# Diffusion backbone with experts: evictions of narrow expert runs queued behind the next wide unit's splits, and regrouped small runs in the mixers

## The chip, the cores and the metric

One core of a Trainium2 chip. The metric is the device time of one execution in microseconds (us); less is better. Engine names are those of the profile: PE is TensorE's matmuls, PEld its weight loads, DVE is VectorE, ACT is ScalarE, POOL is GpSimd, SP is SyncE, whose queue issues the transfers of weights.

## What is computed

Two layers over 256 latent and 256 context tokens of width 1024, float32. Each layer: three token mixers on the same modulated input, gated and merged, then a feed-forward part, dense in layer 0 and eight experts with two per token in layer 1.

```python
def token_mixer(h_lat, h_ctx, lp, need_ctx):
    ...
    out_l = merge_branches(h_lat @ w_gate, (ssd_l, na_l, conf_l)) @ lp['w_o']

def ssd_direction(xs, bm, cm, dt_raw, a_log, dt_bias, h0, reverse):
    ...
    dt = jax.nn.softplus(dt_raw.astype(jnp.float32) + dt_bias.astype(jnp.float32))
    a = -jnp.exp(a_log.astype(jnp.float32))
    y, h = ssd_scan(xs, dt, a, bm, cm, h0)

def moe_swiglu(h, w_router, w_gate, w_up, w_down):
    logits = (h @ w_router).astype(jnp.float32)
    top_v, top_i = lax.top_k(logits, TOP_K)
    top_w = jax.nn.softmax(top_v, axis=-1)
    combine = jnp.sum(jax.nn.one_hot(top_i, N_EXPERTS, ...) * top_w[..., None], axis=-2)
    out = combine[..., 0:1] * swiglu(h, w_gate[0], w_up[0], w_down[0])
    for e in range(1, N_EXPERTS):
        out = out + combine[..., e:e + 1] * swiglu(h, w_gate[e], w_up[e], w_down[e])
    return out
```

## The kernel before

**Big matmuls.** Weights stream from memory through staging buffers on SP's queue (five of 1 MB in the expert stage) and are split into two parts in `split` (L113): ScalarE copies the high part `h_...` (L116), VectorE subtracts to get the low part `l_...` (L117). Three buffers of each are in turn. TensorE then makes three products, high by high, high by low, low by high. In the mixers and the dense feed-forward these are L205 to L207 and L251 to L253, in the experts L1546.

**What sets the order.** The program is written in Python generators and a scheduler with priorities sets each engine's queue. The mixers' small work (attention, the state space part SSD, the conformer convolution, the sums of the conditioning `ada`) runs in jobs that are pumped (`pump`, `spawn`) between the big matmuls: each `yield x` says how much of the big stream shall pass before the job goes on. `defer` keeps a closure of matmuls back for two steps, so that ScalarE and VectorE have made its operands, and `behind()` puts its issue after the last big matmul. Small products take their PSUM tiles from a pool `pw` of four buffers.

**The stages.** Mixers of layer 0 up to about 720 us, dense feed-forward to 1085, mixers of layer 1, routing to 1550, experts from 1550 to 2340 us.

**The mixers' parts.** `dt_path` makes the time steps `dt` of both directions: eight slices of the width, three products each (L865 to L867), with 32 columns. `ada_v` sums conditioning weights on VectorE (`adac`, L374) and then adds up partitions on TensorE with four small matmuls (L382). `attention` transposes the probabilities `P` to `PT` (closure `turned`, a head and a block of queries at a time) and multiplies with the values (`values`). `states` makes SSD chunk states, one direction a closure. `ssd_y` has three closures: `diag` (`ydS`, L1063, masks `MS` from ScalarE L1054 to L1055 and VectorE L1056), `off` (`yoS`, L1080, with `ES` from a DMA and an exponential, L1077) and `fin`.

**The experts.** `moe` (L1294) alternates two generators. `wide()` runs experts 0 to 3 through `expert` and `stream`: units of 1 MB of weights, each split in two halves (`h_er` and so on; tiles `e`, `er` for gate and up, `ed`, `edr` for down). `narrow()` runs experts 4 to 7, up to 64 tokens each, through `expert64` with unsplit float32 weights: runs `nn` (gate and up, L1428) of four units, 32 matmul records in the trace, then down projections `ndn` (L1453). Four narrow units alternate with two wide ones. At the end of an `nn` run ScalarE evicts it to `ntn` (L1433), TensorE transposes that to `npn` (L1438), ScalarE takes a Silu (`nsn`, L1441) and VectorE multiplies (`hnn`, L1443). After the last `ndn` the result is split (`ynHn`, `ynLn`) and combined by `ncn` (L1465). The eviction is issued right behind the run; transposes and what follows wait in the list `later`, which `flush` runs after the next wide unit is issued:

```python
            for _ in islice(w, m):
                self.flush()
```

Of the kernel before, what the change touches and what calls it, by code (L numbers as in the profile page):

```python
# [53 lines left out]
class Body:  # L54
# [298 lines left out]
    def ada_v(self, l, g):  # L353
# [6 lines left out]
        for j0 in (0, 2):  # L360
            accs = []
            for j in (j0, j0 + 1):
# [3 lines left out]
                for k in range(KD):  # L366
# [8 lines left out]
                    yield 0.7 * len(streams)  # L375
                    if j == 1 and k == 0:
                        self.keep()

            ps = self.pw(f"ada{l}{g}{j0}")
            for s in streams:  # L380
                for j, acc in zip((j0, j0 + 1), accs):
                    nc.tensor.matmul(ps[32 * j:32 * j + 32], self.con("oc")[:, 1 - s:33 - s], acc[:, s * 512:(s + 1) * 512],  # L382
                                     start=(s == streams[0]), stop=(s == 1), skip_group_check=True)
# [333 lines left out]
    def attention(self, l, q, kT, v, nt, o_):  # L717
# [4 lines left out]
        q_ = []  # L722
        for q0, nk, lat in streams:
            nkb = nk // 128
            for hp in range(4):
# [5 lines left out]
                def turn(P, j, qb, PT=PT, nm=nm, nk=nk, nkb=nkb, st=st):  # L731

                    nc.vector.tensor_scalar(P, P, st[:, j, qb, 5:6], None, op0=ALU.mult)

                    def turned():
                        if not PT:
                            PT.update({i: self.t4(f"PT{nm}{i}").rearrange("p (k t) -> p k t", t=256) for i in range(2)})
                        pt = self.pw(f"PT{nm}{j}{qb}")
                        for kb in range(nkb):
                            nc.tensor.transpose(pt[:, kb * 128:(kb + 1) * 128], P[:, kb * 128:(kb + 1) * 128], self.con("id"))  # L740
                        ev = nc.scalar.copy if j else nc.vector.tensor_copy
                        ev(PT[j][:, :nkb, qb * 128:(qb + 1) * 128], pt[:, :nk].rearrange("p (k t) -> p k t", t=128))
                    self.defer(q_, turned)
                if lat:
                    for qb in range(2):
# [17 lines left out]
                        for j in range(2):  # L763
                            turn(P[j], j, qb)
                            yield 1.7
                else:
# [6 lines left out]
                    for j in range(2):  # L773
# [5 lines left out]
                        for qb in range(2):  # L779
                            turn(P[j][:, qb * 256:(qb + 1) * 256], j, qb)  # L780
                        yield 1.5
# [7 lines left out]
                self.defer(q_, values)  # L789
                yield 0.5  # L790
        yield from self.undefer(q_)

# [61 lines left out]
    def dt_path(self, l):  # L854
# [3 lines left out]
        wH = self.t2("wdtH" + nm, F32R)[:, :KD * 32].rearrange("p (k n) -> p k n", k=KD)  # L858
# [157 lines left out]
    def ssd_y(self, nm, b, hin, q_):  # L1016
# [23 lines left out]
        for g in range(G):  # L1040
# [6 lines left out]
            for r in range(2):  # L1047
                load(*((1, g) if r == 0 else (0, g + 1)))
                pb = cb[r, g]
                for hq in range(2):  # L1050
# [7 lines left out]
                    def diag(r=r, hq=hq, M=M, g=g, xd=xd, st=st):  # L1058
                        if "pd" not in st:
                            st["pd"] = self.pw(f"yd{nm}{b}{g}")  # L1060
# [751 lines left out]
```

## Time and profile before

| | us |
|---|---|
| median of 3 runs (2364.26 to 2365.93) | 2364.38 |
| the profiled execution's own time | 2367.87 |
| its span, first to last instruction | 2366.1 |
| PE busy, 0 to 720 / 720 to 1085 | 675.64 / 354.72 |
| PE busy, 1085 to 1550 / 1550 to 2340 | 435.05 / 751.12 |
| mean granted clock of TensorE, of full speed | 0.978 |

The page sums the engines over the whole span; the stages differ, so the busy times of TensorE by stage stand beside it. Matmuls are pipelined: a matmul's record is longer than the step to the next one, so the chain of waits, which counts from start to start, gives the price of one in a stream. "Idle before, releaser" in a group of instructions says what an engine waited for ahead of that group; it matters only where the engine is on the chain.

### The profile page before, as it was taken

Reading aid. Unit: us, or ns where it says so; the run is one execution under the profiler, and the core shown is the slowest. Engines: PE = TensorE matmul, PEld = TensorE weight load, DVE = VectorE, ACT = ScalarE, POOL = GpSimd, SP = SyncE. Lnnn points to the kernel's source line nnn. Section 1 sums busy time; section 2 is a strip of 40 time slices with the busy share of each in tenths; the row PEclk is TensorE's granted clock in tenths of the full one; section 3 lists DMA queues with packets and bytes.
Section 4 is the critical chain, followed back from the end, with each engine's and each line's share of the span. In section 5 each row is a group of like instructions: output and inputs, shape, how many; then the busy total and the mean of one; then the engine's idle time right before and its main releaser. Section 6 shows DMA issues by size and latency. Waiting matters only on the chain.

```text
span 2366.1 us, 29723 instructions
## 1 busy us (share of the span) xinstructions
PE 2226.4 (94%) x11075; PEld 1632.5 (69%) x11075; DVE 1509.5 (64%) x2384; ACT 1030.1 (44%) x1658; POOL 17.4 (1%) x32
## 2 busy tenths in 40 slices
PE   7999999699999999999999889899999989999897
PEld 3776677477777777788877779766655656566564
DVE  3667999787667665536898765743433555565556
ACT  4334673643342222225347685443332345454453
POOL 0000000000000000000000000000000000000000
PEclk9999999899999999999999999999999999999998
DMA  7232253445445556423423344488888899999995
GB/s 269 95 117 72 76 172 127 116 156 169 147 143 160 173 175 199 147 98 102 147 89 104 107 146 161 139 324 330 341 320 320 330 365 375 357 385 347 348 370 206
DMA packets 123658, 492.51 MB, mean 208 GB/s; under 512 B 12784, under 2 KB 23792, under 8 KB 89712
## 3 DMA queue, kind: packets, MB, share of 16 engines
q1 hardware_dynamic: 122656, 487.89, 57.4%
q10 hardware_dynamic: 848, 2.62, 0.3%
q8 instruction: 89, 1.46, 0.2%
q14 instruction: 65, 0.53, 0.1%
HBM read 488.24 MB, written 2.23 MB: 207 GB/s over the span
## 4 chain that ended last, share of the span: by engine, by line
PE 71%; issue 11%; DVE 7%; DMA 6%; ACT 4%; POOL 0%; SPq 0%; POOLq 0%; DVEq 0%; ACTq 0%
PE er L1546 8%; PE nn L1428 7%; PE e L1546 4%; DMA adaw<-in_ada_w_dram 4%; PE ndn L1453 4%; PE edr L1546 3%; PE ed L1546 2%; PE wg L205 2%; PE wg L207 2%; PE wg L206 2%; DVE adac L374 2%; PE xbcL L205 1%; PE xbcL L206 1%; PE xbcL L207 1%; PE fu L206 1%
## 5 line engine op out<-in xcount | busy, mean ns | idle before, releaser
L374 DVE SCALAR_TENSOR_TENSOR adac<-adaw,sc,adac 128x512 f32<-128x512 f32 x224 | 160.1, 747 | 57.3 <-DMA adaw<-in_ada_w_dram 56.7
L117 DVE TENSOR_TENSOR l_er<-r_er,h_er 128x1024 fp32r<-128x1024 f32 x132 | 154.5, 1218 | 59.9 <-ACT h_er L116 59.5
L1428 PE MATMUL nn<-r_ngun,xn 128*64 128x512 f32 (+1 forms) x768 | 168.2, 561 | 0.0
L116 ACT ACTIVATE h_er<-r_er 128x1024 fp32r<-128x1024 f32 x132 | 133.0, 1053 | 42.2 <-DMA r_er<-in_moe_gu_dram 29.4
L205 PE MATMUL wg<-hHm,h_wg 128*128 128x512 f32 (+1 forms) x384 | 135.7, 355 | 1.8 <-ACT g L682 1.1
L206 PE MATMUL wg<-hLm,h_wg 128*128 128x512 f32 (+1 forms) x384 | 129.9, 339 | 0.0
L207 PE MATMUL wg<-hHm,l_wg 128*128 128x512 f32 (+1 forms) x384 | 128.8, 339 | 0.5 <-DVE l_wg L117 0.4
L1546 PE MATMUL er<-h_er,gHp 128*128 128x512 f32 (+1 forms) x288 | 110.5, 389 | 17.7 <-ACT h_er L116 17.7
L1428 PEld LDWEIGHTS nn<-r_ngun,xn 128*64 128x64 f32 x768 | 54.2, 137 | 91.9 <-issue 85.1
L1546 PE MATMUL er<-h_er,gLp 128*128 128x512 f32 (+1 forms) x288 | 108.1, 381 | 0.0
L117 DVE TENSOR_TENSOR l_e<-r_e,h_e 128x1024 fp32r<-128x1024 f32 x44 | 52.2, 1222 | 63.5 <-ACT h_e L116 62.6
L1453 PE MATMUL ndn<-r_ndn,hnn 128*64 128x512 f32 x352 | 87.4, 598 | 0.0
L572 DVE SCALAR_TENSOR_TENSOR ccv<-cu,cols,ccv 128x488 f32<-128x488 f32 (+14 forms) x120 | 84.5, 729 | 1.0
L1443 DVE TENSOR_TENSOR hnn<-npn,nsn 128x256 f32<-128x256 f32 (+1 forms) x24 | 9.6, 401 | 117.6 <-ACT nsn L1441 117.6
L1433 ACT ACTIVATE ntn<-nn 128x512 f32<-128x512 f32 (+1 forms) x24 | 13.5, 561 | 162.7 <-PE nn L1428 162.7
L1546 PE MATMUL er<-l_er,gHp 128*128 128x512 f32 (+1 forms) x288 | 84.3, 381 | 0.0
L205 PEld LDWEIGHTS wg<-hHm,h_wg 128*128 128x128 f32 x384 | 72.7, 189 | 14.5 <-issue 4.0
L1546 PEld LDWEIGHTS er<-h_er,gHp 128*128 128x128 f32 x288 | 54.8, 190 | 40.2 <-ACT h_er L116 29.0
L116 ACT ACTIVATE h_wg<-r_wg 128x1024 fp32r<-128x1024 f32 x48 | 50.6, 1058 | 71.8 <-PE wg L206 52.0
L117 DVE TENSOR_TENSOR l_edr<-r_edr,h_edr 128x1024 fp32r<-128x1024 f32 x66 | 77.0, 1217 | 4.4 <-ACT h_edr L116 4.1
L207 PEld LDWEIGHTS wg<-hHm,l_wg 128*128 128x128 f32 x384 | 72.2, 189 | 10.1 <-DVE l_wg L117 2.1
L206 PEld LDWEIGHTS wg<-hLm,h_wg 128*128 128x128 f32 x384 | 72.8, 190 | 8.8 <-issue 2.3
(642 smaller groups left out, 5955.5 us busy)
## 6 DMA issues: line engine op xcount, KB each, us to landing
r_ngun<-in_moe_gu_dram SPq DMA_DIRECT2D x88, 1024.0 KB, 7.1
r_er<-in_moe_gu_dram SPq DMA_DIRECT2D x66, 1024.0 KB, 7.3
r_ndn<-in_moe_down_dram SPq DMA_DIRECT2D x44, 1024.0 KB, 7.6
adaw<-in_ada_w_dram SPq DMA_DIRECT2D x160, 256.0 KB, 3.1
r_edr<-in_moe_down_dram SPq DMA_DIRECT2D x33, 1024.0 KB, 7.4
r_wg<-in_w_in_dram SPq DMA_DIRECT2D x48, 512.0 KB, 3.6
r_e<-in_moe_gu_dram SPq DMA_DIRECT2D x22, 1024.0 KB, 7.6
cbS<-csd SPq DMA_DIRECT2D x24, 512.0 KB, 4.9
```

Source lines behind the costliest of these rows:

```text
L116: nc.scalar.activation(Hd, src, AF.Copy)
L117: nc.vector.tensor_tensor(Ld, src, Hd.bitcast(F32), op=ALU.subtract)
L205: mm(out, wh, xh, start=(first and kk == 0), stop=False, skip_group_check=True)
L206: mm(out, wh, xl, start=False, stop=False, skip_group_check=True)
L207: self.last = mm(out, wl, xh, start=False, stop=(kk == kc - 1), skip_group_check=True).ins
L374: nc.vector.scalar_tensor_tensor(d, w, c, d, op0=ALU.mult, op1=ALU.add)
L572: nc.vector.scalar_tensor_tensor(y[:, :, a:b], x[:, :, a + s:b + s], w[:, k:k + 1], y[:, :, a:b], op0=ALU.mult, op1=ALU.add)
L1428: mm(ps[64 * h:64 * h + 64, :n], x[kk], w[:, h, k, :], start=(kk == 0), stop=(kk == KD - 1), skip_group_check=True)
L1433: nc.scalar.activation(t, ps[:, :n], AF.Copy)
L1443: nc.vector.tensor_tensor(d, v[:, :, 1], g, op=ALU.mult)
L1453: mm(ps[64 * h:64 * h + 64], hT[:, kk * 64:(kk + 1) * 64], w[:, h, k, :], start=(kk == 0), stop=(kk == fc - 1), skip_group_check=True)
L1546: mm(ps[s][j], st[kk], w[p][:, k, :], start=(kk == 0 and p == 0 and q == 0), stop=(kk == kc - 1 and p == 1), skip_group_check=True)
```

## The change

In the experts, the evictions `ntn` and the split of `ynHn`, `ynLn` become closures in a list `evicts`. `stream` runs them behind the second half's split of the next wide unit (`lastH`, set in `split`); `flush` now issues the transposes behind the last wide matmul so far (`last`, set in `stream`). In the mixers, `dt_path` packs high and low weights into 64 columns and makes two products in place of three; `ada_v` waits some more steps before its sums and issues them behind the last big matmul; `attention` transposes both heads in one closure and puts the values with the next one; `states` does both directions in one closure; `ssd_y` has one closure for a direction, which holds what were `diag`, `off` and `fin`; these are kept back one step and not two.

```diff
-        nc.scalar.activation(Hd, src, AF.Copy)
+        self.lastH = nc.scalar.activation(Hd, src, AF.Copy).ins
...
-                    yield 0.7 * len(streams)
+                    yield 0.64 * len(streams)
...
+            yield len(streams)
             ps = self.pw(f"ada{l}{g}{j0}")
-            for s in streams:
-                for j, acc in zip((j0, j0 + 1), accs):
-                    nc.tensor.matmul(ps[32 * j:32 * j + 32], self.con("oc")[:, 1 - s:33 - s], acc[:, s * 512:(s + 1) * 512],
+            with self.behind():
+                for s in streams:
+                    for j, acc in zip((j0, j0 + 1), accs):
+                        nc.tensor.matmul(ps[32 * j:32 * j + 32], self.con("oc")[:, 1 - s:33 - s], acc[:, s * 512:(s + 1) * 512],
...
+                        pts = [self.pw(f"PT{nm}{j}{qbs[0]}") for j in range(2)]
+                        n = len(qbs) * 128
+                        for f in joined:
+                            f()
+                        joined.clear()
...
+                    self.defer(q_, turned, 1)
...
-            nc.tensor.matmul(ps[0:32, :], wH[:, k, :], self.h[0][k], start=(k == 0), stop=False)
-            nc.tensor.matmul(ps[0:32, :], wH[:, k, :], self.h[1][k], start=False, stop=False)
-            nc.tensor.matmul(ps[0:32, :], wL[:, k, :], self.h[0][k], start=False, stop=(k == KD - 1))
+            nc.tensor.matmul(ps[0:64, :], wp[:, k, :], self.h[0][k], start=(k == 0), stop=False, skip_group_check=True)
+            nc.tensor.matmul(ps[0:32, :], wp[:, k, 0:32], self.h[1][k], start=False, stop=(k == KD - 1), skip_group_check=True)
...
+        nc.vector.tensor_tensor(b3(x), pt[:, :, 1], bc(self.col("dtb")), op=ALU.add)
+        nc.vector.tensor_tensor(b3(x), pt[:, :, 0], b3(x), op=ALU.add)
...
+                def state(g=g, xe=xe):
+                    ps = {r: self.pw(f"st{nm}{b}{r}{g}") for r in dirs}
...
+                self.defer(q_, state, 1)
+                yield 1.8 * len(dirs)
...
+                def diag(r=r, M=M, g=g, xd=xd, st=st, E=E):
+                    if r == 0:
+                        st["pd"] = self.pw(f"yd{nm}{b}{g}")
+                    E = {d: e.rearrange("p i l -> p (i l)") for d, e in E.items()}
+                    for e in E.values():
+                        nc.scalar.activation(e, e, AF.Exp)
+                    for hl in range(8):
+                        nc.tensor.matmul(st["pd"][64 * (hl % 2):64 * (hl % 2) + 64, (hl // 2) * 128:(hl // 2 + 1) * 128],
...
+                    po = {d: self.pw(f"yo{nm}{b}{g}{d}") for d in E}
...
+                self.defer(q_, diag, 1)
+                yield 1.8 if r == 0 else 4.2
...
             for _ in islice(w, m):
-                self.flush()
+                self.flush(self.last)
+            self.evict()
...
+    def evict(self, ins=None):
+
+        f, self.evicts = self.evicts, []
+        if f:
+            with self.tc.issue_after(ins) if ins is not None else ExitStack():
+                for g in f:
+                    g()
...
                 if (i + 1) * nk == KD:
+                    self.evict()
                     self.flush()
                     t = self.t2(f"nt{nm}{c}")[:, :n]
-                    with self.prio("ev"):
-                        nc.scalar.activation(t, ps[:, :n], AF.Copy)
+
+                    def evicted(t=t, ps=ps, n=n):
+                        with self.prio("ev"):
+                            nc.scalar.activation(t, ps[:, :n], AF.Copy)
+                    self.evicts.append(evicted)
...
                     w = self.weight(None, f"{name}{i}_{s}", t=t[:, s * 1024:(s + 1) * 1024])
+                if s:
+                    self.evict(self.lastH)
```

How the order of instructions moves, at three places. The first is ScalarE's queue around the end of the narrow run `nn70`, the stop at 2115 us in the trace. `h_er242` and `h_er243` are the high halves of the next two wide units, `ntn70` is the eviction. Before:

```order
L116 ACTIVATE hHr2_15825<-etr230_16307 128x512
L1433 ACTIVATE ntn70_16395<-nn70_16370 128x512
L1441 ACTIVATE nsn70_16424<-npn70_16419 128x256
L116 ACTIVATE h_er242_0_16399<-r_er242_16397 128x1024
L116 ACTIVATE h_er242_1_16409<-r_er242_16397 128x1024
L116 ACTIVATE h_er243_0_16429<-r_er243_16427 128x1024
L116 ACTIVATE h_er243_1_16441<-r_er243_16427 128x1024
```

After:

```order
L116 ACTIVATE hHr2_15793<-etr230_16275 128x512
L116 ACTIVATE h_er242_0_16366<-r_er242_16364 128x1024
L116 ACTIVATE h_er242_1_16376<-r_er242_16364 128x1024
L1466 ACTIVATE ntn70_16363<-nn70_16338 128x512
L116 ACTIVATE h_er243_0_16397<-r_er243_16395 128x1024
L116 ACTIVATE h_er243_1_16409<-r_er243_16395 128x1024
L1475 ACTIVATE nsn70_16392<-npn70_16387 128x256
```

The eviction moved from ahead of the splits of unit 242 to behind both of them.

The same place in TensorE's queue, before:

```order
L1428 MATMUL nn70_16370<-r_ngun71_16377,xn_12733 64x512 x4
L1428 MATMUL nn70_16370<-r_ngun72_16383,xn_12733 64x512 x4
L1428 MATMUL nn70_16370<-r_ngun73_16389,xn_12733 64x512 x4
L1438 MATMUL npn70_16419<-con_t_98,ntn70_16395 128x128 x4
L1546 MATMUL er240_0_16314<-h_er242_0_16399,gHp0_14651 128x512
L1546 MATMUL er240_0_16314<-h_er242_0_16399,gLp0_14652 128x512
L1546 MATMUL er240_0_16314<-h_er242_0_16399,gHp0_14651 128x512
```

After:

```order
L1458 MATMUL nn70_16338<-r_ngun73_16357,xn_12701 64x512 x4
L1586 MATMUL er240_0_16282<-h_er242_0_16366,gHp0_14619 128x512
L1586 MATMUL er240_0_16282<-h_er242_0_16366,gLp0_14620 128x512
L1586 MATMUL er240_0_16282<-h_er242_0_16366,gHp0_14619 128x512
L1586 MATMUL er240_0_16282<-h_er242_0_16366,gLp0_14620 128x512
L1586 MATMUL er241_0_16283<-h_er242_1_16376,gHp0_14619 128x512
L1586 MATMUL er241_0_16283<-h_er242_1_16376,gLp0_14620 128x512
L1586 MATMUL er240_0_16282<-l_er242_0_16367,gHp0_14619 128x512 x2
L1586 MATMUL er241_0_16283<-h_er242_1_16376,gHp0_14619 128x512
L1586 MATMUL er241_0_16283<-h_er242_1_16376,gLp0_14620 128x512
L1586 MATMUL er241_0_16283<-l_er242_1_16377,gHp0_14619 128x512 x2
L1472 MATMUL npn70_16387<-con_t_98,ntn70_16363 128x128 x4
```

The transposes `npn70` moved from the end of the narrow run to behind unit 242's first twelve rows, which now follow the run at once.

The third place is TensorE's queue at the layer 0 conformer's output product `wb0conf_out`, around 450 to 465 us; `ydS` are products of `ssd_y`, `ada010` the row sums. Before:

```order
L1063 MATMUL ydS020_3352<-MS02010_3345,xdS0201_3269 64x128 x4
L1063 MATMUL ydS020_3352<-MS02011_3383,xdS0201_3269 64x128 x4
L1063 MATMUL ydS021_3555<-MS02100_3484,xdS0210_3478 64x128 x4
L382 MATMUL ada010_3621<-adac010_2977,con_t_98 32x512
L382 MATMUL ada010_3621<-adac011_3328,con_t_98 32x512
L382 MATMUL ada010_3621<-adac010_2977,con_t_98 32x512
L382 MATMUL ada010_3621<-adac011_3328,con_t_98 32x512
L205 MATMUL wb0conf_out0_0_3571<-c0_0_3305,h_wb0conf_out0_0_3577 128x512
L206 MATMUL wb0conf_out0_0_3571<-cL_3304,h_wb0conf_out0_0_3577 128x512
```

After, the start of that product:

```order
L1094 MATMUL ydS020_3371<-MS02010_3325,xdS0201_3253 64x128 x4
L1094 MATMUL ydS020_3371<-MS02011_3358,xdS0201_3253 64x128 x4
L1094 MATMUL ydS021_3552<-MS02100_3439,xdS0210_3433 64x128 x4
L1094 MATMUL ydS021_3552<-MS02101_3462,xdS0210_3433 64x128 x4
L205 MATMUL wb0conf_out0_0_3568<-c0_0_3286,h_wb0conf_out0_0_3574 128x512
L206 MATMUL wb0conf_out0_0_3568<-cL_3285,h_wb0conf_out0_0_3574 128x512
L207 MATMUL wb0conf_out0_0_3568<-c0_0_3286,l_wb0conf_out0_0_3575 128x512
```

and 13 rows further on:

```order
L205 MATMUL wb0conf_out0_2_3570<-c0_0_3286,h_wb0conf_out0_0_3574 128x512
L206 MATMUL wb0conf_out0_2_3570<-cL_3285,h_wb0conf_out0_0_3574 128x512
L207 MATMUL wb0conf_out0_2_3570<-c0_0_3286,l_wb0conf_out0_0_3575 128x512
L384 MATMUL ada010_3596<-adac010_2953,con_t_98 32x512
L384 MATMUL ada010_3596<-adac011_3264,con_t_98 32x512
L384 MATMUL ada010_3596<-adac010_2953,con_t_98 32x512
L384 MATMUL ada010_3596<-adac011_3264,con_t_98 32x512
L1053 MATMUL scS03_3615<-uL0_10_1134,uL0_8_1133 128x128 x2
```

The four row sums moved from ahead of the conformer's product to behind its first 18 matmuls, and the four `ydS` pieces stand together ahead of it.

## Rows read from the trace of the kernel before

**Rows 1.** Parts 1, 4 and 5 of the page: engines, chain, one group of instructions.

```profile
PE 2226.4 (94%) x11075; PEld 1632.5 (69%) x11075; DVE 1509.5 (64%) x2384; ACT 1030.1 (44%) x1658; POOL 17.4 (1%) x32
...
PE 71%; issue 11%; DVE 7%; DMA 6%; ACT 4%; POOL 0%; SPq 0%; POOLq 0%; DVEq 0%; ACTq 0%
...
L1433 ACT ACTIVATE ntn<-nn 128x512 f32<-128x512 f32 (+1 forms) x24 | 13.5, 561 | 162.7 <-PE nn L1428 162.7
```

**Rows 2.** Waits of TensorE, 1550 to 2340: who for whom, total us, times, longest.

```profile
PE er L1546 <- ACT h_er L116: 17.7, 18, 1.6
PE npn L1438 <- ACT ntn L1433: 10.0, 15, 0.7
PE edr L1546 <- ACT h_edr L116: 4.8, 6, 1.4
```

**Rows 3.** Chain of waits, 1560 to 1628: start us, us, what.

```profile
1565.54 0.44 PE npn L1438 x4
...
1570.54 7.02 PE nn L1428 x32
1577.56 4.77 PE e L1546 x20
...
1606.65 7.04 PE nn L1428 x32
...
1613.72 0.60 ACT ntn L1433
...
1614.37 0.67 PE npn L1438 x4
...
1615.34 1.06 ACT h_e L116
...
1616.44 9.60 PE e L1546 x34
```

**Rows 4.** Chain of waits, 2216 to 2232: the last stop of this size.

```profile
2217.16 7.04 PE nn L1428 x32
...
2226.95 5.06 PE er L1546 x14
```

**Rows 5.** Chain of waits, 1629 to 1640: the milder form.

```profile
1629.93 7.03 PE nn L1428 x30
...
1638.58 1.43 PE e L1546 x5
```

**Rows 6.** Chain of waits, 1680 to 1700: as many matmuls with no stop ahead.

```profile
1686.91 7.93 PE e L1546 x34
```

**Rows 7.** Windows: length, busy us of each engine, PEclk, DMA share, GB/s.

```profile
1880.00:2320.00 440.00, 409.59 (x1855) 257.65 (x1853) 240.09 (x248) 206.55 (x249) 0.00 (x0) 0.99 0.94 364
...
1950.00:2000.00 50.00, 45.19 (x222) 29.05 (x220) 25.09 (x27) 22.97 (x29) 0.00 (x0) 1.00 0.97 371
...
2050.00:2100.00 50.00, 48.58 (x206) 30.03 (x205) 31.62 (x32) 26.33 (x29) 0.00 (x0) 1.00 0.99 396
...
2228.00:2231.00 3.00, 3.00 (x9) 2.35 (x8) 3.00 (x4) 1.73 (x2) 0.00 (x0) 0.50 1.00 423
...
440.00:450.00 10.00, 2.73 (x32) 1.96 (x30) 4.25 (x8) 8.52 (x18) 0.00 (x0) 0.79 0.70 166
```

**Rows 8.** Chain of waits, 88 to 104: one time step product.

```profile
90.22 0.23 PE dt L865
```

**Rows 9.** Waits of TensorE, 0 to 720, then 720 to 1085.

```profile
PE wb0conf_out L205 <- ACT g L682: 11.4, 1, 11.4
...
PE ada L382 <- DVE adac L374: 7.0, 9, 1.7
```

**Rows 10.** Timeline of TensorE, 447 to 454; table loads in the groups of ScalarE.

```profile
450.36 3.05 PE L382 MATMUL ada<-adac,con_t 128*32 128x512 f32 x8
...
L682 ACT ACT_TABLE_LOAD x16 | 20.5, 1283 | 0.3
```

**Rows 11.** Tile `ydS`: what TensorE waited for ahead of it, us, times.

```profile
  DVE MS L1056: 14.3, 6
```

More of the change, by code (lines that the diff above doesn't have):

```diff
@@ L762, in attention @@
                         nc.vector.reciprocal(s[:, :, 5], s[:, :, 5])
-                        for j in range(2):
-                            turn(P[j], j, qb)
-                            yield 1.7
+                        turn([{qb: p} for p in P], (qb,))
+                        yield 3.4
                 else:
@@ L778, in attention @@
                         nc.vector.reciprocal(st[:, j, :, 5], st[:, j, :, 5])
-                        for qb in range(2):
-                            turn(P[j][:, qb * 256:(qb + 1) * 256], j, qb)
-                        yield 1.5
+                        yield 1.2
+                    turn([{qb: p[:, qb * 256:(qb + 1) * 256] for qb in range(2)} for p in P], (0, 1))
+                    yield 0.6
                 def values(hp=hp, PT=PT, nm=nm, nkb=nkb, q0=q0):
@@ L788, in values @@
                     self.split(po[:, 0:256], o_[0][hp][:, q0:q0 + 256], o_[1][hp][:, q0:q0 + 256])
-                self.defer(q_, values)
-                yield 0.5
+                self.defer(q_, lambda f=values: joined.append(f), 1)
         yield from self.undefer(q_)
+        yield 1.0
+        with self.behind():
+            for f in joined:
+                f()
     def conv31(self, cu, cv, nt):
@@ new lines, in ssd_y @@
+                    nc.scalar.activation(m, m, AF.Exp, scale=-1.0)
+                    nc.vector.tensor_tensor(m, m, scm[:, r, g, None, :].to_broadcast([128, 4, 128]), op=ALU.mult)
+                    if hq == 0:
+                        yield 1.8
+                E = {}
+                for d in range(2) if r else ():
+                    if hin[d] is None:
+                        continue
+                    E[d] = self.t2(f"E{nm}{b}{g}{d}").rearrange("p (i l) -> p i l", i=4)
+                    for j in range(2):
+                        nc.sync.dma_start(E[d][64 * j:64 * j + 64], rows(d, g).rearrange("(i j) l -> j i l", j=2)[j][None].to_broadcast([64, 4, 128]))
@@ L1348, in moe, with flush @@
                     self.final()
-    def flush(self):
-        for f in self.later:
-            f()
-        self.later = []
+    def flush(self, ins=None):
+        f, self.later = self.later, []
+        if f:
[4 more added lines that the diff above has]
+        f, self.evicts = self.evicts, []
+        if f:
+            with self.tc.issue_after(ins) if ins is not None else ExitStack():
+                for g in f:
+                    g()
     def others(self, pairs):
@@ L1445, in expert64 @@
                 yield True
+        self.evict()
         self.flush()
@@ L1454, in expert64, with evicted @@
             if i == fc // 2 - 1:
[L1455 to L1457 removed]
+                y = [self.p2.tile([128, 512], F32R, name=f"yn{p}{nm}", tag="yn" + p, bufs=1) for p in "HL"]
+                def evicted(ps=ps, y=y):
+                    with self.prio("ev"):
+                        self.split(ps, *y)
+                self.evicts.append(evicted)
                 def combined():
```

118 lines of the change are left out of this document (49 added, 69 removed).

## The prediction

> **What bounds the kernel now.** I read the page first [rows 1]. TensorE is busy 94% of the span, and the chain that ended last lies on it for 71%; the rest is issue, VectorE, DMA and ScalarE in small shares. So the kernel is TensorE's work plus its holes, and an edit is worth the holes that it closes on that engine, the matmuls that it takes off it, and nothing else. The page also names where one hole comes from: `ntn`, the eviction of a narrow run (L1433), is the ScalarE group with the most idle time ahead of it, 162.7 us, all of it waiting for the end of `nn`. ScalarE takes its queue in order; whatever stands behind `ntn` waits with it.
>
> Then the waits of TensorE in the expert stage [rows 2]: 17.7 us for the high half `h_er` in 18 waits, 4.8 for `h_edr` in 6, and 10.0 us of the transposes `npn` for `ntn` in 15. The longest are 1.6, 1.4 and 0.7 us: one mechanism, many times.
>
> The chain of waits shows it [rows 3]. The narrow run ends at 1613.69; `ntn` takes 0.60, `npn` 0.67, and only then comes the split `h_e`, 1.06, which was ready to go long before but stood behind `ntn`. The wide run starts at 1616.44, 2.75 us after the narrow one (2.77 by the matmuls' own ends). The last of this size is at 2224.20 to 2226.95 [rows 4]. A milder form has the high half split already, and stops for eviction and transposes alone: 1636.96 to 1638.58 [rows 5]. Where no eviction stands between, the wide run follows without a gap: 1570.54 plus 7.02 is 1577.56, the next start [rows 3].
>
> **The change part by part, experts.** I counted the stops at the end of narrow runs: 10 of 2.77 us (1606 the first, 2217 the last), 5 of 1.64 (first 1629), 2 of 2.23 for half-width runs, 2 of 2.07 where a narrow down projection ends and `ncn` follows. That is 27.7 + 8.2 + 4.5 + 4.1 = 44.5 us. In the new order ScalarE has both splits of the next wide unit ahead of `ntn`, and TensorE has that unit's first 12 rows between `nn` and `npn`; every narrow run is followed by a wide one at once, as at 1577.56.
>
> What comes back: the transposes are still done, now amid wide matmuls, where four cost 0.44 (`npn` at 1565.54 [rows 3]). 15 x 0.44 + 2 x 0.22 = 7.0. `ncn`, partly inside the hole now, keeps about 1.1 each, 2.2; gate products that stand in two of the holes keep about 0.9. Together 10.2, so 44.5 - 10.2 = 34.3 us. The added wait is `ntn` behind two splits. Behind it on ScalarE stand the splits of the unit after the next; a wide unit keeps TensorE 4.77 us for 20 matmuls of `e` [rows 3], and `ntn` takes 0.60, so this is covered as long as the next unit's data has landed. If it has not, ScalarE waits at the split with `ntn` behind it, but TensorE then waits for the same split anyway.
>
> The clock: after the hole at 1613 the 34 matmuls of `e` took 9.60 us, at 1686, without one, 7.93 [rows 3, 6]: 1.67 more. The granted clock after the hole at 2224 is 0.50 for three microseconds [rows 7], which is the lower of the two levels, 1.2 GHz. I find four such stretches behind the holes (1616, 1801, 2118, 2227), 4 x 1.65 = 6.6 us, and they go with the holes.
>
> What is late next is the transfer of weights. From 1880 to 2320 the DMA queues move 364 GB/s with a share of 0.94; the best 50 us there, 2050 to 2100, have 396 GB/s with TensorE busy 48.58 of 50 [rows 7]. Of the gain above, 32.9 us of holes less 8.0 of moved work plus 3.2 of clock, 28 us, lie in these 440 us. Without them the same bytes have to come in 412 us, 364 x 440 / 412 = 389 GB/s. This is under the 396 that one window held, but so near to it that late units will cost something; at a steady 396 the stretch could not go below 404 us. I deduct 8 us, bounds 0 and 28 (nothing gained there). By the Trainium skill, "DMA: Bandwidth & Descriptors", section "Where 436 GB/s comes from", transfers from HBM are bound at about 358 GB/s for each NeuronCore, with 435 the ceiling of the fabric. By that rule the whole stretch would be at its bound already and the 28 us lost; the 396 GB/s that the trace holds for 50 us speaks against it, so it is a rival and not the forecast.
>
> Experts: 34.3 + 6.6 - 8 = 33 us, bounds 13 and 41.
>
> **The change part by part, mixers.** *Time steps* (L865 to L867): 24 matmuls a layer become 16, 16 fewer in all, each 0.23 in the chain [rows 8]: 3.7 us. The first of each pair now has 64 weight columns; the rows show the same 0.23 for products with 128. The added VectorE addition is off the path. *Row sums of ada* (L382): in the dense FFN TensorE waits 7.0 us in 9 waits for VectorE's `adac` [rows 9], because the sums stand right behind the last accumulation. Put off by the added yield they stand 26 to 36 big matmuls later, but only half of the groups move whole (the others keep their pairs apart): I take 4.5, bounds 0 and 7. *Merged runs* (attention, states, `ssd_y`): 35 fewer interruptions of the big streams, no matmul less. A small matmul amid big ones costs 0.11 (four for 0.44 [rows 3]); I take half of that for an interruption, 2 us, bounds 0 and 3.9. *A stall that stays*: in layer 0 TensorE waits 11.4 us for the conformer's `g` [rows 9], while it is busy 2.73 of 10 us from 440 to 450 [rows 7]. ScalarE is what is late, with 8.52 us of work in these 10 us, and its order there hardly changes. But four row sums now done inside this stall, 3.05 us from 450.36 [rows 10], come behind the conformer's first 18 matmuls: 3 us lost. Three table loads more on ScalarE, 1.28 each [rows 10], are the bound of a loss here, 3.9; the stall itself, 11.4, that of a gain. I take 0. The Trainium skill, "ScalarE: Activation LUTs", section "What ACT_TABLE_LOAD costs", counts 2.66 us for a load with its drain; the 0.3 us of idle time ahead of 16 loads in the row shows no such drain. By the page that loss would be 8.0 instead of 3.9. The stalls of `ydS` for the masks `MS` (14.3 us in 6 waits, both layers [rows 11]) stay, since the masks are still made by the same ScalarE and VectorE steps; 0.
>
> Mixers: 3.7 + 4.5 + 2 - 3 = 7 us, bounds -3 (3.7 - 3 - 3.9) and 26 (3.7 + 7 + 3.9 + 11.4).
>
> **Sum.** 33 + 7 = 40 us off the profiled span of 2366.1, which gives 2326. The profiled execution's own time is 2367.9, 1.8 above its span, and 3.5 above the median of the runs, 2364.4. Less 40 the median becomes 2324.
>
> **Rivals.** *The weights take over.* If the stretch from 1880 to 2320 is already at what the queues sustain, its 28 us turn from a wait for `h_er` behind `ntn` into a wait for `h_er` behind `r_er`. For it: the share of 0.94 at 364 GB/s, and 371 from 1950 to 2000 with TensorE busy only 45.19 of 50 [rows 7]. Against: 396 in the window where TensorE is busy 48.58, so the rate follows TensorE there and not the other way round. Then 41 - 28 = 13 for experts and 7 for mixers: 2344.
>
> *The holes get shorter but stay.* The new order helps only if both splits of the next unit are done when the narrow run ends. Their data come through five staging buffers that narrow units share; where the unit behind the run has not landed, TensorE waits up to a landing. From the trace the next unit's data was there ahead of nearly all holes, since the split ran at once after `ntn`; if a third of the stops stay, with their moved work, 11 to 13 us are lost: 2336.
>
> *Slower than before: the mixers' small PSUM pool.* The merged closures of `ssd_y` hold a diagonal tile and two off-diagonal ones while the next group's transposes take another: all four buffers of `pw`. Every merged closure can then hold TensorE until VectorE has read the tiles. The price from the row: 14.3 us in 6 waits [rows 11], 2.4 each, and 24 merged closures (192 matmuls of `ydS` in the trace, 8 to a closure) make 57 us against a gain of 40: 2381. It decides from the 17th closure that stalls. Against it: they stand behind big matmuls in the order, which cover VectorE's reading, and only 6 such waits are there now.
>
> *The mixers' part does not do what it says.* The two stalls of layer 0 move with the conformer's ScalarE work, and if the merged `ssd_y` brings that forward, up to 11 us are won: 2313. If it holds it back, 2332.
>
> **How the numbers follow.** The forecast, 2312 to 2334, 0.68. The weights take over, 2344: 0.12. Holes stay, 2336: 0.08. Layer 0 better or worse, 2305 to 2312 and 2334 to 2340: 0.07. PSUM pool, 2381: 0.04. The last 0.01 is for the unknown. The range reaches from 2304, the better layer 0 with little late data, to 2346, the weights' case: about 0.85 of the chances lie in it. A measurement of this kernel can tell about 0.2%, some 5 us. Faster by more than that: all but the pool and half of what is unknown, 0.94. Within: 0.02, a weights' case with bad mixers. Slower: 0.04.
>
> **What would show it.** In the profile after: `npn` and `h_er` gone from TensorE's waits in the expert stage (from 32.5 us for the three of rows 2 to well under half); the idle time ahead of `ntn` no longer on `nn` alone; the wide runs after narrow ones starting with no gap; the DMA rate from the stage's middle on near 390 GB/s; where a unit is late, L1546 waits for a split that itself waits for a DMA. In the mixers: 32 matmuls of `dt` for 48, the waits of `ada` for `adac` halved, 11 us for `g` in layer 0 still there. It is wrong if the rate in that stretch stays at 364 to 371 while TensorE waits for `h_er`, or if `ydS`, `yoS` or the transposes wait for VectorE in layer 0 more than the 14.3 us of both layers now.

## The result, and the profile after

The changed kernel takes 2295.4 us (median of 4 runs, 2289.6 to 2297.6) against 2364.3 before: ratio 0.971, interval 0.969 to 0.973. That is 69 us less. The forecast was 40 less, with 2304 as the lower end, so the direction is right and the size is not. Measured twice more, it took 2295.0 and 2294.2.

One warning for everything below. Runs of one kernel differ by up to 16 us (the kernel before by 13.5, 2353.7 to 2367.2 in 25 runs), and the profiled executions lie anywhere in that: 2367.9 for the kernel before, 2289.6 for the changed one. So their traces stand 78 us apart where the medians stand 69.

The page of the changed kernel: the engines, the granted clock in 40 slices, the rate of the transfers, the chain that ended last.

```profile
PE 2180.8 (95%) x11059; PEld 1617.5 (71%) x11059; DVE 1509.9 (66%) x2382; ACT 1035.0 (45%) x1657; POOL 17.4 (1%) x32
...
PEclk9999999799999999999999999989999999999999
...
GB/s 274 103 115 85 79 163 141 83 174 158 171 151 166 166 179 206 176 94 91 147 115 83 99 162 150 199 221 340 351 337 350 318 391 395 398 393 389 384 383 230
...
PE 72%; issue 10%; DVE 9%; DMA 5%; ACT 3%; POOL 0%; SPq 0%; POOLq 0%; DVEq 0%; ACTq 0%
```

TensorE has 45.6 us less busy time at hardly fewer matmuls (11059 for the 11075 of [rows 1]), and 33 us fewer holes. From the 28th slice on, the last one aside, the transfers run at 318 to 398 GB/s.

The waits of TensorE in the expert stage (who for whom, total us, times, longest):

```profile
PE er L1586 <- ACT h_er L116: 7.3, 11, 0.7
PE edr L1586 <- ACT h_edr L116: 0.7, 2, 0.3
```

Of [rows 2], `npn` for `ntn` is gone, `er` fell from 17.7 to 7.3 and `edr` from 4.8 to 0.7. Ten of the 11 waits left of `er` are stops of 0.5 to 0.7 us behind another eviction, `esr`, which the change does not touch; the eleventh, 0.47 us at 2155, is for a split whose data had come late. On ScalarE in the same stretch:

```profile
ACT h_er L116 <- DMA r_er<-in_moe_gu_dram: 84.0, 19, 9.8
...
ACT nsn L1475 <- PE npn L1472: 33.8, 19, 2.7
...
ACT ntn L1466 <- PE nn L1458: 32.6, 15, 4.3
```

Before, `ntn` was ScalarE's largest wait with 162.7 us [rows 1]; now it is 32.6, and ScalarE's splits wait for data instead, 84.0 us, but for that one place early enough for TensorE. The chain of waits, at the place of the stop of 2.77 us that the order listing showed:

```profile
2046.51 0.44 PE etr L1634 x4
2046.95 2.52 PE er L1586 x11
2049.47 7.02 PE nn L1458 x32
2056.49 2.95 PE er L1586 x12
2059.44 0.44 PE npn L1472 x4
2059.88 2.30 PE er L1586 x10
```

The narrow run of 7.02 us is followed by the wide run at once, and four transposes stand amid it for 0.44, as in [rows 3].

### The profile page after: what moved, and what is told of

It reads as the page before. It is cut to its first block, busy times and chain, and to the rows that moved or that the text cites. A ratio compares the mean times of both kernels' runs of the same rounds, so it can differ in the third digit from the quotient of the medians.

```text
span 2287.7 us, 29706 instructions
## 1 busy us (share of the span) xinstructions
PE 2180.8 (95%) x11059; PEld 1617.5 (71%) x11059; DVE 1509.9 (66%) x2382; ACT 1035.0 (45%) x1657; POOL 17.4 (1%) x32
## 4 chain that ended last, share of the span: by engine, by line
PE 72%; issue 10%; DVE 9%; DMA 5%; ACT 3%; POOL 0%; SPq 0%; POOLq 0%; DVEq 0%; ACTq 0%
PE er L1586 7%; PE nn L1458 7%; PE e L1586 5%; PE edr L1586 4%; PE ndn L1488 4%; DMA adaw<-in_ada_w_dram 3%; PE ed L1586 2%; DVE ccv L574 2%; PE wg L205 2%; PE wg L207 2%; PE wg L206 2%; PE fd L252 1%; PE fd L253 1%; PE fu L206 1%; PE fd L251 1%
## 5 line engine op out<-in xcount | busy, mean ns | idle before, releaser
L574 DVE SCALAR_TENSOR_TENSOR ccv<-cu,cols,ccv 128x482 f32<-128x482 f32 (+14 forms) x120 | 85.2, 729 | 1.1
L116 ACT ACTIVATE h_edr<-r_edr 128x1024 fp32r<-128x1024 f32 x66 | 67.0, 1055 | 34.5 <-DMA r_edr<-in_moe_down_dram 28.3
L205 PE MATMUL xbcL<-hHm,h_xbcL 128*128 128x512 f32 (+1 forms) x192 | 75.8, 395 | 0.0
```

Source lines behind the costliest of these rows:

```text
L116: self.lastH = nc.scalar.activation(Hd, src, AF.Copy).ins
L205: mm(out, wh, xh, start=(first and kk == 0), stop=False, skip_group_check=True)
L574: nc.vector.scalar_tensor_tensor(y[:, :, a:b], x[:, :, a + s:b + s], w[:, k:k + 1], y[:, :, a:b], op0=ALU.mult, op1=ALU.add)
```

## The experiments

The parts of the change were put into the kernel before one by one and in company, and taken out of the changed kernel. The table has stretches of TensorE, in us, from the first matmul of one product to the first of the next, read from the trace of each kernel (`xbcL` to `wg` is most of layer 0's attention, `fg`, `fu` and `fd` are the dense feed-forward's gate, up and down products, `e` and `er` the two halves of the wide experts; a 1 marks layer 1). Where it says late, the mark is not the product's first matmul but a later one, the 169th of `xbcL` 1, the 121st of `wg` 1 and the 25th of `zL` 1; the end of `edr` is its 361st of 396. Between traces of identical code most of these stretches differ by up to 1.5 us; `woL` to `fg` (not shown), `fd` to `xbcL` 1, `e` and `er` by up to 5.

| stretch | before | after | attention alone | row sums alone | `ssd_y` alone | time steps, states alone | after, states of before |
|---|---|---|---|---|---|---|---|
| `xbcL` to `wg` | 105.4 | 97.4 | 97.4 | 105.4 | 105.4 | 105.4 | 97.4 |
| `wb0na_out` to `wb0conf_out` | 120.8 | 118.3 | 119.8 | 120.4 | 115.4 | 123.4 | 112.5 |
| `wb0conf_out` to `zL` | 32.2 | 34.5 | 32.1 | 35.9 | 34.3 | 32.1 | 34.0 |
| `zL` to `wb0ssd_out` | 110.1 | 106.6 | 110.1 | 110.2 | 108.8 | 111.1 | 107.2 |
| `fg` to `fd` | 105.6 | 95.4 | 105.8 | 96.9 | 105.5 | 109.8 | 95.3 |
| `fd` to `xbcL` 1 (late) | 446.9 | 450.2 | 443.8 | 446.6 | 445.2 | 444.6 | 446.8 |
| `xbcL` 1 (late) to `wg` 1 (late) | 66.6 | 67.3 | 70.0 | 66.2 | 67.4 | 68.8 | 66.5 |
| `wb1na_out` to `zL` 1 (late) | 68.1 | 63.3 | 68.0 | 66.2 | 66.5 | 69.2 | 64.5 |
| `zL` 1 (late) to `wb1conf_out` | 23.5 | 21.1 | 23.5 | 23.5 | 21.1 | 23.5 | 21.1 |
| `e` to `er` | 300.7 | 288.1 | 300.8 | 297.5 | 299.3 | 299.2 | 288.1 |
| `er` to the end of `edr` | 476.3 | 444.2 | 479.5 | 477.5 | 476.3 | 477.6 | 444.5 |

**Experts alone** (`e1_experts`): the kernel before with `evicts`, `lastH` and `last` only.

```diff
                     w = self.weight(None, f"{name}{i}_{s}", t=t[:, s * 1024:(s + 1) * 1024])
+                if s:
+                    self.evict(self.lastH)
```

> The kernel before with the experts' part of the change alone. The prediction's steps say 33 us less than before, since it took 8 us off for weights that come late. The rival, that the weights have reserve left, says 41 to 45 us less, a DMA rate of about 390 GB/s from the middle of the expert stage on, and no wait of TensorE behind a split that waits for its data.

2314.6 us, ratio 0.981 (0.978 to 0.984), 45 to 47 less. In its trace the two expert stretches are 12.6 and 32.2 us shorter, the same as in the changed kernel. The rival holds but for one place: a single wait of TensorE, 0.5 us, is for a split whose data came late.

**What the transfers can do** (`m4_no_low`): products of the low weights in the wide experts left out.

```diff
-                for p in range(2):
+                for p in range(1):
```

> The changed kernel without the products of the low weights in the wide experts, a third of their matmuls left out (the splits remain), so that TensorE no longer sets the pace. It measures the rate at which weights can come at all. The prediction's deduction of 8 us and its rival need a ceiling at or just above 390 GB/s; if the ceiling is 420 or more, the weights had reserve in the change and the deduction had no ground. Time between 1820 and 2260 of the changed kernel shrinks in that ratio, and TensorE waits for splits that wait for data.

One run, 2228.2 us. Four windows of its expert stage (length, busy us of PE, PEld, DVE, ACT, POOL, granted clock, DMA share, GB/s), then TensorE's waits there:

```profile
1850.00:1900.00 50.00, 42.56 (x198) 22.46 (x197) 27.03 (x29) 23.59 (x29) 0.00 (x0) 1.00 1.01 417
1900.00:1950.00 50.00, 41.73 (x190) 23.89 (x187) 32.94 (x34) 28.29 (x34) 0.00 (x0) 1.00 1.01 417
1950.00:2000.00 50.00, 43.20 (x177) 23.36 (x176) 34.63 (x35) 28.72 (x32) 0.00 (x0) 1.00 1.01 421
2000.00:2050.00 50.00, 44.48 (x226) 26.32 (x226) 29.84 (x36) 24.50 (x36) 0.00 (x0) 1.00 1.01 420
```

```profile
PE er L1586 <- ACT h_er L116: 23.5, 24, 2.0
PE edr L1586 <- ACT h_edr L116: 11.9, 14, 1.7
```

With TensorE no longer setting the pace the queues sustain 417 to 421 GB/s in these windows, share 1.01 (416 over the 330 us from 1820 to 2150), and now TensorE does wait for splits; 21 of the 24 waits of `er` are for splits that themselves waited for data. The changed kernel needs less, in the stretch that answers to 1880 to 2320 of [rows 7]:

```profile
1820.00:2260.00 440.00, 431.94 (x1980) 276.48 (x1979) 267.20 (x278) 225.89 (x268) 0.00 (x0) 1.00 0.97 388
```

388 GB/s, which is the 389 that the prediction had worked out as the need, and 7 to 8% under what the queues did there. It has little late data, but some: the place at 2155 comes back at 2146 to 2179 in all but one of the other kernels that have the experts' change and all products, with up to 1.0 us, and with 2.2 in the second repeat of the changed kernel (`q2_after`):

```profile
PE er L1586 <- ACT h_er L116: 9.3, 12, 2.2
```

**Attention alone** (`e2_attention`): both heads' transposes in one closure, values with the next one.

```diff
-                def turn(P, j, qb, PT=PT, nm=nm, nk=nk, nkb=nkb, st=st):
+                def turn(P, qbs, PT=PT, nm=nm, nk=nk, nkb=nkb, st=st):
...
-                self.defer(q_, values)
-                yield 0.5
+                self.defer(q_, lambda f=values: joined.append(f), 1)
```

> The kernel before with the change of attention alone. The prediction's price for a merged run, some 0.06 us each, says about 1 us less. The rival: products that use half of TensorE's array (S with 64 rows, po with 64 columns) run two at a time when they stand next to each other in the queue, and the old order tore the pairs apart. It says 8 to 13 us less, of it about 8 on S and 4 on po.

2358.2 us, ratio 0.998 (0.997 to 1.000): 3 us less, less than the rival said. But the table shows its stretch 8.0 us shorter, as in every kernel that has it, and 3.4 given back from `xbcL` to `wg` in layer 1 (late marks). Chains of waits of the kernel before and, below, of the changed one, one pair of heads in layer 0:

```profile
168.06 0.44 PE PT L740 x4
...
171.38 0.63 PE S L770 x2
172.01 0.26 PE PT L740
172.27 1.06 PE S L770 x6
173.32 0.37 PE PT L740 x2
173.69 0.58 PE po L786 x2
174.27 0.43 PE xbcL L205
174.70 1.01 PE po L786 x6
```

```profile
167.50 0.87 PE PT L751 x8
168.37 1.06 PE S L781 x8
...
173.78 1.01 PE po L797 x8
```

A product of `S` or `po` leaves two records here, and the two heads' products use different halves of the array. Before, one product of `S` alone (two records) took 0.63 and three in a row 1.06; now four in a row take 1.06. Among the three there was a neighbour on the other half to run beside; the one, with a transpose behind it, had none. The prediction read none of this: its price was that of a 128-wide transpose.

**Torn pairs** (`m3_by_head`): the changed kernel with the loops of context scores and of values turned.

```diff
-                    for kb in range(nkb):
-                        for j in range(2):
+                    for j in range(2):
+                        for kb in range(nkb):
                             mm(po[64 * j:64 * j + 64, 0:256], ...
```

> The changed kernel with the same attention products in another order: for context scores and for values all of one head first, then all of the other. No product more, no closure less. If neighbours on different halves of the array run together, this tears the pairs apart and costs 12 to 22 us over the changed kernel: po from about 0.13 to 0.21 us or more a record, context S from 0.13 to 0.2. If a small product costs the same next to any other, the time is that of the changed kernel.

2298.2 us, 3 more than the changed kernel, within what runs differ by; the expected 12 to 22 did not come. The trace says why: in short runs (two products of one head, two of the other) next to nothing changes, `po` x8 takes 1.02 for 1.01 and `S` x8 1.07 for 1.06. In the runs of 16 records it does. The same 16 of `po`, changed kernel and this one:

```profile
227.09 1.95 PE po L797 x16
```

```profile
227.55 2.86 PE po L797 x16
```

All of `po` takes 26.8 us instead of 20.8 (from start to start over the trace), and `xbcL` to `wg` 99.2 instead of 97.4. So neighbours on different halves do run together. That the short runs do not change fits a partner that may stand a product or two further on; a transpose in between ends it, as the lone `S` shows.

**Row sums alone** (`e3_ada`).

```diff
+            yield len(streams)
             ps = self.pw(f"ada{l}{g}{j0}")
-            for s in streams:
+            with self.behind():
+                for s in streams:
```

> The kernel before with the put-off row sums alone. The prediction says 1 to 2 us less (4.5 won in the dense feed-forward, 3 lost at the layer 0 conformer). The rival, that the four sums also run two at a time when they stand together, says 5 to 9 us less, most of it between 705 and 810 us, and a sum that costs 0.23 us a record in place of 0.34 or more.

2362.1 us, ratio 1.000 (0.999 to 1.001): nothing. The table has 8.7 us won from `fg` to `fd` and 3.7 lost behind the conformer; the rest is little more than traces of one kernel differ by. The timeline of TensorE (start, length, idle time ahead in brackets) in the kernel before, one sum that stands alone and two that stand together, and in the changed kernel, four of them together, each with the big product that follows:

```profile
777.04 1.05 PE L382 MATMUL ada<-adac,con_t 128*32 128x512 f32 x2 [1.67 <-DVE adac L374]
778.02 0.50 PE L205 MATMUL fg<-hHf,h_fg 128*128 128x512 f32 x1
...
800.85 1.05 PE L382 MATMUL ada<-adac,con_t 128*32 128x512 f32 x4 [0.76 <-DVE adac L374]
801.83 0.50 PE L205 MATMUL fu<-hHf,h_fu 128*128 128x512 f32 x1
```

```profile
749.46 1.91 PE L384 MATMUL ada<-adac,con_t 128*32 128x512 f32 x8
751.30 0.50 PE L205 MATMUL fg<-hHf,h_fg 128*128 128x512 f32 x1
```

A sum leaves two records. Up to the start of the next product, one sum alone keeps TensorE 0.98 us, behind a wait of 1.67; two together also 0.98, four 1.84. These sums use 32 columns each at different places of the array, and run two at a time when they stand side by side.

**All but the row sums** (`m2_but_ada`).

> The changed kernel with the row sums of before. Alone the put-off sums were worth nothing, what the dense feed-forward gained (9 us in the trace) was lost at the layer 0 conformer and elsewhere. If this holds in company, this kernel takes as long as the changed one, within 3 us. If the merged closures cover the loss, it is 6 to 10 us slower than the changed one.

2301.5 us, 6 more than the changed kernel. From `fg` to the first `ggL` of layer 1, which is the whole dense feed-forward, it takes 398.7 us, as before, and the three traces of the changed kernel take 390.7, 393.5 and 393.5: in company the sums are worth what the feed-forward shows.

**Closures of `ssd_y` alone** (`e4_ssd_y`).

```diff
-                    self.defer(q_, diag)
-                    yield 1.8
...
-                self.defer(q_, off)
-                yield 1.2
...
+                self.defer(q_, diag, 1)
+                yield 1.8 if r == 0 else 4.2
```

> The kernel before with the merged closures of ssd_y alone. The prediction says about 1 us less, with the waits of ydS for the masks unchanged. The rival that remains from before, the four buffers of the small PSUM pool, says slower by 5 us or more. A third, that fewer switches between small and big products also free the stretches behind them, says 3 to 6 us less, in layer 1 above all.

2356.0 us, ratio 0.998 (0.996 to 0.999): 5.5 less. The pool of four buffers is no bound that shows. The stretches with the stalls that the prediction kept are shorter: 2.4 us less from the late `zL` 1 to `wb1conf_out` in every kernel that has this part and in no other, 5.4 less ahead of the layer 0 conformer, of which 2.1 are given back behind it.

**Time steps and states alone** (`n1_dt_states`): two products for three, and

```diff
-                    self.defer(q_, state)
-                    yield 1.8
+                self.defer(q_, state, 1)
+                yield 1.8 * len(dirs)
```

> The kernel before with the two-pass time steps and the joined chunk states alone. By the prediction 3.7 us less for the 16 matmuls and next to nothing for the states: 3 to 5 us less. If the parts of the mixers simply add up to the 26 us that they win together, this one has to bring 14 or more, since the other three brought 12.

2366.6 us, ratio 1.002 (1.001 to 1.003): 4 us slower, where 3 to 5 less had been expected. The 16 matmuls are gone, 3.7 us by the trace (48 records of 0.23 became 32), but the stretch ahead of the conformer grows by 2.6, `fg` to `fd` by 4.2 and layer 1 by 3.

**The mixers together** (`m1_mixers`), attention with states and `ssd_y` (`n2_att_ssd`), row sums with `ssd_y` (`n3_ada_ssd`).

> The whole change but the experts' part. The prediction's sum for the mixers is 7 us less. The parts run so far add up to about 12 less (attention 3, merged closures of ssd_y 5.5, two-pass time steps 3.7 by the trace, row sums nothing). If the parts help each other, 18 to 24 less: the stalls that attention alone or the row sums alone brought (about 4 us each) are gone when all are in.

> The kernel before with attention, chunk states and the merged closures of ssd_y, without time steps and row sums. Parts that only add up give 9 to 10 us less. If attention's loss in layer 1 alone (4 us of waiting of PT) goes away in company, 13 to 16 less, and the stretch from the last xbcL products to the next gates is no longer than before.

> The kernel before with the put-off row sums and the merged closures of ssd_y. Parts that only add up give 5 us less. If the merged closures cover the place where the put-off sums lose at the layer 0 conformer, 9 to 14 less.

2336.5 us (0.989, 0.986 to 0.992), 26 less; 2349.9 (0.996), 12 less; 2346.9 (0.993), 15 less. Alone the four bring 3, 0, 5.5 and -4, together 26 with an interval of 19 to 34. So most of the mixers' gain is not a sum of parts.

**The changed kernel again** (`n4_after`, and `q2_after` below).

> The changed kernel once more, beside the others on one chip: 2293 to 2300 us, 64 to 70 less than before. Its second trace tells which differences between two traces are the clock's alone; if the stages of the same code differ by up to 3 us from trace to trace, differences of that size in single traces tell nothing of a part.

2295.0 us. Against the first trace of the same code, one stretch (`woL` to `fg`) differs by 3.4 us and `fd` to `xbcL` 1 by 2.3; the second repeat differs by 3.3 in the latter and by 3.9 from `er` on. That is the size below which a single trace tells nothing of these stretches.

**Taken out of the changed kernel**: states (`p1_no_states`), attention (`p2_no_attention`), both (`p3_exp_ada_ssd_dt`).

> The changed kernel with the chunk states of before (one direction a closure). Time steps and joined states alone made the kernel slower by 4 us, and the stretches around the layer 0 conformer are 5 us shorter in the kernel that has row sums and ssd_y only. If the joined states are what costs there, this one beats the changed kernel by 3 to 6 us; if they pay through later stretches, as the layer 1 attention output suggests (63 us with them, 66 without), it is 2 to 5 us slower.

> The changed kernel with the attention of before. If attention is worth the 8 us that its layer 0 stretch shows in every kernel that has it, this one takes 8 to 12 us longer than the changed kernel. If it is worth the 3 us that it brought alone, 2 to 4.

> The changed kernel with attention and chunk states of before. If parts add up from here on, its loss is the sum of the two others' losses. If the two help each other in layer 1, it is less than that sum, by 2 to 4 us.

2284.5, 2294.4 and 2297.3 us. Without the joined states the kernel is 10 us faster (its four runs spread from 2280.9 to 2297.1); without the new attention it is as fast as with it, although `xbcL` to `wg` then takes 105.4 again; without both it is within what runs differ by. The parts do not add up here either: attention is worth 12 to 13 us when the states are apart, and nothing measurable when they are joined. TensorE's waits in layer 0, in the changed kernel and in the one with the states of before:

```profile
PE wb0conf_out L205 <- ACT g L684: 12.9, 1, 12.9
...
PE ydS L1094 <- DVE MS L1075: 7.3, 4, 3.3
```

```profile
PE yoS L1097 <- DVE hsS0l L982: 7.0, 1, 7.0
PE wb0conf_out L205 <- ACT g L684: 5.4, 1, 5.4
```

The conformer's output product waited 12.9 us for ScalarE's `g`; with the states apart it waits 5.4, and 7.0 more stand at `yoS`, for the chunk states themselves. The stretch ahead of `wb0conf_out` falls from 118.3 to 112.5.

Where attention gives its 8 us back can be seen in part. TensorE's waits from 1200 to 1300 us, the attention of layer 1, in the changed kernel and in the one with the attention of before:

```profile
PE PT L751 <- DVE P L737: 3.8, 1, 3.8
PE PT L751 <- ACT P L770: 3.2, 2, 2.8
```

```profile
PE PT L742 <- DVE P L735: 4.0, 2, 3.4
```

The second wait, of the transposes for ScalarE's exponentials, is in all three traces of the changed kernel (2.8 to 3.2 us) and in none with the attention of before. From the first `ggL` of layer 1 to the late `xbcL` these three take 154.5 to 154.8 us, 6.8 of them at a granted clock of 0.50; with the attention of before it is 151.2 and 151.3, none at that clock. That is 3 to 4 of the 8 us. The wait is there with the states apart too (2.9 and 3.0), so it does not explain why attention is worth more in that company.

**A version that beats both** (`q1_no_states`), beside the changed kernel (`q2_after`).

> The changed kernel with the chunk states of before once more, against the changed kernel in the same call. Its trace showed 6 us less between the layer 0 attention output and the conformer output (112.5 against 118.3 us) and its median 11 less. If that is the kernel and not the run, the same stretch is again 112 to 113 us and the median again 5 to 11 us below the changed kernel's.

> The changed kernel beside it: 2293 to 2298 us, the stretch before the conformer output again 118 us.

2285.3 us (5 runs, 2285.1 to 2296.7, ratio 0.968 to before, 0.965 to 0.970) against 2294.2 (2292.2 to 2298.7, 0.968 to 0.973): again 9 less in the median, the stretch 113.7 against 118.4. The runs of the two kernels overlap, but the median came out 9 to 10 lower both times. The whole change without the joined closures of `states` is the fastest kernel here.

## Why the prediction was wrong

**Experts, forecast -33, measured -45 to -47.** The mechanism was right. The 44.5 us of stops went, every narrow run is followed without a gap, the transposes cost 0.44 amid wide matmuls, and in the trace of the changed kernel the four stretches at the lower clock went with the stops. The step that failed is the deduction of 8 us for weights that come late. The need of 389 GB/s was right to 1 (388 measured); what was wrong is the ceiling. The prediction took the best window of before, 396 [rows 7], for the most that the queues give. But there too TensorE set the pace, so that row was a lower bound of the ceiling; `m4_no_low` puts it at 417 to 421. Late data cost TensorE 0.5 us in the kernel with the experts' part alone and 2.2 at that place in a repeat of the whole change, so the deduction should have been near 0, its own bound. By the Trainium skill, "DMA: Bandwidth & Descriptors", section "Where 436 GB/s comes from", 358 GB/s would bind here; the same page's section "Bandwidth" gives that as the part of each of two cores that stream at once, and has 425 measured for a transfer of 16 MB by one core alone. These runs of one core show up to 421.

Without the deduction the prediction's terms give 41, by stretch 12.8 up to `er` (44.5 - 32.9 of holes, less 10.2 - 8.0, and 3.4 of clock) and 28.1 from there on. Measured are 12.6 and 32.2. The 4 us more lie from `er` on: about 1 in stops, transposes and combines, 3 in the steps of the big products themselves, beyond what the clock term had for them; why is not known. A trace has its own count of stretches at the lower clock: `e` to `er` takes 300.7 in the trace of before, with two of them, and 297.5 in `e3_ada`, the same code there, with none.

**Mixers, forecast -7, measured -20 to -26.** Three steps failed, and parts that were added up do not add up.

*Merged runs, 2 us.* The prediction priced an interruption by a transpose of 0.11 us, without looking at the products that were interrupted. In layer 0 alone attention gained 8.0 us: 5.4 on `S`, 2.6 on `po` and 1 on `PT`, by the time from start to start, less 1 on the big products. The price was in the trace of before, `S` x2 in 0.63 beside `S` x6 in 1.06. The Trainium skill, "TensorEngine Tiling (Array Packing)", section "Key Properties", has the rule that was not looked for: tiles of the array run independently, and a change of the tiling mode drains the engine. The trace agrees with the first, by 1.95 us for 16 records of `po` in turn and 2.86 by head; no run here sets the drain apart.

*Row sums, 4.5 us less 3.* The net of 1.5 came out as 0 alone and 6 in company. The loss behind the conformer came in the kernel with the row sums alone, 3.7 us for the 3 that were forecast; in company it did not, `wb0conf_out` to `zL` takes 34.5 in the changed kernel and in the one with the row sums of before. The gain was 10.2 from `fg` to `fd`; with what is given back behind `fd`, where one group of sums has moved, it is 5 to 8 over the whole feed-forward, for 4.5. The prediction counted the waits and not that sums side by side take 0.46 us each in place of 0.98.

*Stalls of `ydS` and the rest, 0.* The prediction argued that the masks are made by the same steps as before, and so the stalls stay. The waits for `MS` did stay, 12.1 us for the 14.3 of [rows 11]. But the closures stand at other places in the big stream, and stretches around them became shorter by 3.5 (`zL` to `wb0ssd_out`), 4.8 (`wb1na_out` to the late `zL` 1) and 2.4 us (that to `wb1conf_out`), in kernels that have `ssd_y`'s closures, the first two in full only together with the others: 10.7 us together, where the prediction had 0.

Right were the time steps, 3.7 us, the layer 0 stall that stays (12.9 for 11.4 us), and the pool of four PSUM buffers, which does not show as a bound. The three table loads more on ScalarE came too, 66 for 63; that they cost nothing is not shown.

**The range.** The bounds of the two sums, 41 and 26, reached down to 2297. The range ended at 2304, since it took the bounds of unknown costs as unlikely where nothing spoke for the middle. The experts' 45 to 47 lie above even their bound of 41.

**What stays open.** Why the parts help or hinder each other is shown only by stretches: states joined cost 5 us ahead of the layer 0 conformer, and attention's 8 us, less 3 to 4 in layer 1, are seen in the time only when they are apart. One thing goes with it: between the last `wg` product and the first of `wb0conf_out` ScalarE makes six table loads of 1.28 us in each of the three traces of the changed kernel, where this takes 28.3 us, and four in both traces with the states apart, where it takes 20.2. That the order in which the pumped jobs' steps reach ScalarE and VectorE, and the table loads that it brings, make `g` late is argued, not shown.

## What to carry to other kernels

An eviction that waits for a product blocks all that stands behind it on its engine: queue it behind the work that TensorE needs next, and leave it as late as its own reader allows. A rate seen while another engine sets the pace is a lower bound of what the queues can do; measure the ceiling with that engine out of the way before a gain is cut for it. Count the price of small products by their shape and by their neighbours, and test joined steps in company, since parts that gain alone can take back each other's gain.

## What the runs showed of the hardware

- Products at different places of the array run together when they stand close in the queue: 16 records of 64 columns in 1.95 us in turn, 2.86 us with one half's records first; of sums with 32 columns one takes 0.98 us, two 0.98, four 1.84.
- A single core's queues sustained 416 GB/s over 330 us from memory with transfers of 1 MB, 417 to 421 in windows of 50 us, share 1.01.
- Runs of the same code differ by 13 to 16 us of about 2300; traces of the same code agree to 0.1 us where TensorE is kept busy (69.6 to 69.7 us from `qL` to `xbcL` in all of them) and by up to 5 in stretches with waits.
